# A hybrid decoder layer on one core: the attention's value products of both query groups stand behind the transposes and masked copies of both groups

## The chip, the cores and the metric

The kernel runs on one core of a Trainium2 chip. The metric is the device time of one execution in microseconds (us), and lower is better. The kernel before took 2198.51 us as the median of three runs, which lie between 2198.18 and 2198.69 us. The engines are named as in the profile: PE does matrix products (PEld is its weight load), DVE and ACT do elementwise work, POOL and SP do almost none here beside constants and the issue of transfers.

## The reference

One decoder layer works on 2048 tokens of width 1024. After an RMSNorm and an input projection, four heads of a gated linear recurrence (HGRN2) and eight heads of sliding-window attention run side by side on the same input; their outputs, put side by side, pass an output projection and are added to the residual. A gated MLP with a short causal convolution follows, and a last RMSNorm. The part that the change touches is the attention:

```
scores = jnp.einsum('bnqhgd,bnkhd->bnhgqk', qb, kb) * scale
scores = jnp.where(mask[None, :, None, None], scores, -jnp.inf)
m = jnp.maximum(jnp.max(scores, axis=-1, keepdims=True), sink)
p = jnp.exp(scores - m)
denom = jnp.sum(p, axis=-1, keepdims=True) + jnp.exp(sink - m)
out = jnp.einsum('bnhgqk,bnkhd->bnqhgd', p / denom, vb)
```

Each block of 128 queries reads its own block of 128 keys and the one before it. The recurrence runs beside it:

```
decay = jnp.exp(jnp.where(causal, rel, -jnp.inf))
scores = jnp.einsum('bhtk,bhsk,bhtsk->bhts', qi, ki, decay)
intra = jnp.einsum('bhts,bhsv->bhtv', scores, vi)
inter = jnp.einsum('bhtk,bhkv->bhtv', qi * jnp.exp(b), state)
```

## The kernel before

The 2048 tokens are worked in two halves of 1024. For each half there is first a mixing stage (the loop at line 1187 up to line 1227), then the output projection (`out_proj`), then the gate and up products (`gate_up`), then the down product (`down`). Every large float32 product is made of three products of a high and a low part (hi·hi, hi·lo, lo·hi), so a projection of 128 output columns over 1024 inputs and 1024 tokens is a `unit` (line 194): 8 input tiles (kt) times 3 products times 2 halves of 512 tokens, 48 matmuls of 128x512. In the mixing stage the units f, hq, g (recurrence), q (attention) and, for pairs of heads, pvv (values) fill PE; the output projection's units are called pop. PE executes what it is given in order, and so do DVE and ACT.

In the mixing stage one loop pass per head index h runs two generators side by side, `hgrn` for recurrence head h and `attend` for the head pair (h, h+4) of the attention, and calls `next` on them in a fixed pattern of steps (lines 1198 to 1226). The written order gives each instruction its rank; a scheduler, which runs when the program is built and simulates the engines' times, sets the order on every engine by that rank and by what it thinks ready (`schedule_with_timeline_sim=True`, line 1290). So the place of a `yield` moves ranks, and the built order shows where the instructions went.

`attend` has these parts:

- The q unit, scaled and biased into `qT`, and a `yield`.
- For each of two groups g of four query blocks: the high and low parts `qh` and `ql` (tag `pp`), the score products psc (L459), the copies into `sc`, the row maximum, the exponentials (L481, each 128x128), the division by the sum (L486). Then a `yield`.
- For each group: four transposes of `sc` into the bank ppt (L495) for each of two key/value heads, the masked copies `po` and `pp` from it (L498, tag `pp`, four buffers), the 16 value products into the bank poT (L506; 14 for the very first group), and the copy out of poT: L510 for h below 3; for h = 3, where the result goes straight into the output projection, the high part XH on ACT (L516) and the low part XL on DVE (L517). A `yield` after each group.

The banks psc, ppt, poT and pv share one tag `at` with two buffers in PSUM, and `out_proj` takes both of them for its third unit (d = 2).

`hgrn` walks seven levels m = 1, 2, 4, ... 64 (line 590). At each level PE makes plev from Q and K (L569 for heads 0 to 2, L602 and L607 for head 3), and then DVE changes Q and K in place (L609, L610), which the next level's products read; a masked copy (L625) places the result into `ST`. After the levels come the transposes pkn of K (L640), the copy `Kn` on ACT (L641), the products pu (L647), a chain of eight small sums SS on DVE (L651), the output products po (L665, L666) with a square on ACT for each (L667), a short series of tiny DVE operations for the inverse root (`rsqrt`, line 160), the scaling `on` (L674), the transposes pot (L679), and the result `hg` (L680), which for head 3 is split into XH (L683) and XL (L684).

The output projection's units read the eight mixed tiles in the order kt = 0, 4, 1, 5, 2, 6, 7, 3. Tile 7 comes from the attention of head index 3, and tile 3 from the recurrence of head 3. So in the pass h = 3 the units pop of d = 0, 1 (`pop_3557` and `pop_3558`, `pop_3626` and `pop_3627` in the first half) can run before the mixing is done, except for their steps kt = 7 and kt = 3, and d = 2 (`pop_3697`, `pop_3698`) is tied by the table `BEHIND` (line 38) to stand behind pu, po and pot at its steps 0, 2 and 5.

Of the kernel before, what the change touches and what calls it, by code (L numbers as in the profile page):

```python
# [8 lines left out]
F32 = mybir.dt.float32  # L9
F32R = mybir.dt.float32r  # L10
# [7 lines left out]
P = 128  # L18
# [26 lines left out]
WARM = 12  # L45
TAIL_WARM = 7
LV = 4


@with_exitstack  # L50
def hymba_layer(ctx: ExitStack, tc: tile.TileContext, a: dict, out: bass.AP):
    nc = tc.nc

    def pool(name, bufs=1, space=None, stack=ctx, **kw):
        if space is not None:
            kw["space"] = space
        return stack.enter_context(tc.tile_pool(name=name, bufs=bufs, **kw))
# [12 lines left out]
    def ps(kind, name):  # L70
        return spaces[kind].tile([P, 512], F32, tag=kind, name=name)
# [3 lines left out]
    def halves():  # L75
        return [(b, slice(b * 512, (b + 1) * 512)) for b in range(NB)]
# [117 lines left out]
    def unit(src, X, name, order=range(KT), kind="mm", then={}, behind={}, in_turn=False):  # L194


        hi, lo = src if isinstance(src, tuple) else prep(src)
        o = [ps(aux[b] if kind == "aux" else kind, f"{name}{b}") for b in range(NB)]
        order, mark = list(order), None
        for both in [[h] for h in halves()] if in_turn else [halves()]:  # L200
            for i, kt in enumerate(order):
                if i in then:
                    then[i]()
                wh, wl = hi[:, kt * P:(kt + 1) * P], lo[:, kt * P:(kt + 1) * P]
                xh, xl = X[kt]
                if i in behind:
                    mark = marks[behind[i]].ins
                with tc.issue_after(mark) if mark else ExitStack():
                    for w, x, f, l in ((wh, xh, kt == order[0], False), (wh, xl, False, False),
                                       (wl, xh, False, kt == order[-1])):  # L210
                        for b, bs in both:
                            marks["unit"] = nc.tensor.matmul(o[b], w, x[:, bs], start=f, stop=l)  # L212
        return o

    def new_x():
        return (xp.tile([P, HALF], F32R, tag="xh", name="XH", bufs=KT),
                xp.tile([P, HALF], F32R, tag="xl", name="XL", bufs=KT))
# [74 lines left out]
    def slot(name):  # L292
        return hp.tile([P, HALF], F32, tag="m", name=name, bufs=KT)
# [102 lines left out]
    def rows(kv):  # L396
        return slice(kv * HD, (kv + 1) * HD)
# [32 lines left out]
    def attend(hf, j, X, invb, KS, V, mix, p):  # L430

        o = unit(a["w_att"][j], X, "q")
        qT = slot(f"att{j}")
        for b, bs in halves():
            nc.vector.scalar_tensor_tensor(qT[:, bs], o[b], 0.125, invb[:, bs], op0=ALU.mult, op1=ALU.mult)
            nc.scalar.activation(qT[:, bs], qT[:, bs], AF.Identity, bias=C.bq[:, j:j + 1])
        yield
        scs = []
        for g in range(NB):
            sc = p.tile([P, 2, 4, P], F32, tag="sc", name="sc", bufs=2)  # L440
            gs = slice(g * 512, (g + 1) * 512)
            for kv in range(2):
                r, other = rows(kv), rows(1 - kv)

                qh, ql = [p.tile([P, 512], F32R, tag="pp", name=n, bufs=4) for n in ("qh", "ql")]
                nc.scalar.copy(qh[r], qT[r, gs])
                nc.scalar.copy(qh[other], qT[r, gs])
                nc.vector.tensor_tensor(ql[r], qT[r, gs], qh[r].bitcast(F32), op=ALU.subtract)
                nc.scalar.copy(ql[other], ql[r].bitcast(F32))
                for i0 in (0, 2):  # L450
                    pb = ps("at", "psc")
                    first = hf == 0 and g == 0 and i0 == 0
                    for i in range(2):
                        n = g * 4 + i0 + i
                        w0 = 1 if first and i == 0 else 0
                        o = pb[:, i * 256 + w0 * P:(i + 1) * 256]
                        ks = slice((n + w0) * P, (n + 2) * P)
                        for t, qx in enumerate((qh, ql)):
                            nc.tensor.matmul(o, qx[:, (i0 + i) * P:(i0 + i + 1) * P], KS[:, kv, ks],  # L459
                                             start=t == 0, stop=t == 1)  # L460
                    pv = pb.rearrange("p (i w k) -> p i w k", i=2, w=2)
                    dst = sc[:, kv, i0:i0 + 2]
                    if first:
                        nc.vector.memset(dst[:, 0], NEG)
                        nc.scalar.copy(dst[:, 1], pv[:, 1, 0])
                    else:
                        nc.scalar.copy(dst, pv[:, :, 0])
                    nc.vector.copy_predicated(
                        dst, C.own.bitcast(U32).unsqueeze(1).to_broadcast([P, 2, P]), pv[:, :, 1])
            m = p.tile([P, 2, 4], F32, tag="mx", name="m", bufs=2)  # L470
            nc.vector.tensor_reduce(m.rearrange("p a b -> p (a b)"),
                                    sc.rearrange("p a b c -> p (a b) c"), axis=AX.X, op=ALU.max)
            sk = C.sinkb[:, j].unsqueeze(2).to_broadcast([P, 2, 4])
            nc.vector.tensor_tensor(m, m, sk, op=ALU.max)
            es = p.tile([P, 2, 4], F32, tag="es", name="es", bufs=2)
            nc.vector.tensor_tensor(es, sk, m, op=ALU.subtract)
            nc.vector.tensor_scalar(m, m, -1.0, None, op0=ALU.mult)
            den = p.tile([P, 2, 4], F32, tag="den", name="den", bufs=2)
            for kv in range(2):
                for i in range(4):  # L480
                    nc.scalar.activation(sc[:, kv, i], sc[:, kv, i], AF.Exp, bias=m[:, kv, i:i + 1],  # L481
                                         accum_out=den[:, kv, i:i + 1])
            nc.scalar.activation(es, es, AF.Exp)
            nc.vector.tensor_tensor(den, den, es, op=ALU.add)
            nc.vector.reciprocal(den, den)
            nc.vector.tensor_tensor(sc, sc, den.unsqueeze(3).to_broadcast([P, 2, 4, P]), op=ALU.mult)  # L486
            scs.append(sc)
        yield
        for g, sc in enumerate(scs):
            pm = []  # L490
            for kv in range(2):
                pm.append([p.tile([P, 4, P], F32, tag="pp", name=n, bufs=4) for n in ("po", "pp")])
                pt = ps("at", "ppt")
                for i in range(4):
                    nc.tensor.transpose(pt[:, i * P:(i + 1) * P], sc[:, kv, i], ident)  # L495
                ptv = pt.rearrange("p (i q) -> p i q", i=4)
                for dst, mk in zip(pm[kv], (C.ownT, C.prevT)):
                    nc.vector.tensor_tensor(dst, ptv, mk.unsqueeze(1).to_broadcast([P, 4, P]), op=ALU.mult)  # L498
            oT = ps("at", "poT")
            for i in range(4):  # L500
                n = g * 4 + i
                noprev = hf == 0 and n == 0
                for prev in range(1 if noprev else 2):
                    for kv in range(2):
                        r = rows(kv)
                        nc.tensor.matmul(oT[r, i * P:(i + 1) * P], V[:, n + 1 - prev, r], pm[kv][prev][:, i],  # L506
                                         start=prev == 0, stop=noprev or prev == 1)
            gs = slice(g * 512, (g + 1) * 512)
            if j < ATT_J - 1:
                nc.scalar.copy(qT[:, gs], oT)  # L510
                mix[4 + j] = qT
            else:
                if g == 0:
                    mix[4 + j] = new_x()
                h, l = mix[4 + j]
                nc.scalar.copy(h[:, gs], oT)  # L516
                nc.vector.tensor_tensor(l[:, gs], oT, h[:, gs].bitcast(F32), op=ALU.subtract)  # L517
            yield

    def hgrn(hf, h, X, invb, vs, WG, mix, p, fu=None):  # L520

# [50 lines left out]
        def place_pairs():  # L572

            plv = pl.rearrange("p (r c t) -> p r c t", r=TT // 2, c=2)
            moved, odd = [p.tile([P, TT // 2, 64], F32, tag="lv", name=n, bufs=LV) for n in ("moved", "odd")]
            nc.scalar.copy(moved, plv[:, :, 1])
# [610 lines left out]
    for hf in range(NH):  # L1187
        X, kv, invb, rs, f0 = nxt
        with ExitStack() as st:
            p = pool(f"mix{hf}", stack=st, reuse_waits="tile")  # L1190
# [37 lines left out]
        with ExitStack() as st:  # L1228
            p = pool(f"ffn{hf}", stack=st, reuse_waits="tile")
# [64 lines left out]
```

## Time and profile before

| | |
|---|---|
| timed runs | 2198.18 to 2198.69 us, median 2198.51 |
| profiled execution, first to last instruction | 2198.0 us (its own time is not given apart from this span) |
| PE busy | 2180.4 us, 99% |
| DVE busy | 1639.5 us, 75% |
| ACT busy | 1049.9 us, 48% |
| chain that ended last | PE 95%, DVE 3%, ACT 1%, DMA 1% |
| heads 0 to 2 of the mixing, from the first plev to the first pop | 90.2 to 334.2 us and 1180.0 to 1424.6 us |
| head 3, with the output projection's first three units, to the first pop of the fourth | 334.2 to 404.2 us and 1424.6 to 1494.2 us |

In the profile's lists a line reads: start in us, duration in us, engine, line of the kernel, operation, out<-in, shape, how many of them in a row, and in brackets how long the engine sat idle before it and what ended that. Matmuls overlap by their pipeline, so the distance from start to start tells what one costs. A float32 product of small tiles appears as two records. A list by windows shows for each stretch its length and the busy time of the engines in it, with the number of instructions, and then the granted TensorE clock (PEclk) as a share of the full one.

### The profile page before, as it was taken

The page shows a single profiled execution, that of the slowest core. Times are in us where ns is not written, and L with a number is a line of the kernel's source. Part 1 is how long each engine was busy: PE and PEld are TensorE (multiplying, and loading weights), DVE is VectorE, ACT ScalarE, POOL GpSimd, SP SyncE. Part 2 cuts the span into 40 slices and gives each one's busy share as a digit, 9 for nine tenths or more (in the row PEclk, how much of TensorE's full clock was granted, in tenths as well). Part 3 has the DMA queues.
Part 4 walks back from the last instruction along what each step waited for, and adds up shares of the span by engine and source line. Part 5 has one row for each costly group of instructions (what it writes and reads, how often), then busy time and mean ns, then how long its engine had stood idle before and what let it go on. Part 6 is the DMA issues. An engine that isn't in the chain of part 4 may idle for free.

```text
span 2198.0 us, 29524 instructions
## 1 busy us (share of the span) xinstructions
PE 2180.4 (99%) x11424; PEld 1834.0 (83%) x11424; DVE 1639.5 (75%) x2451; ACT 1049.9 (48%) x1848; POOL 6.3 (0%) x28
## 2 busy tenths in 40 slices
PE   9999999999999999999999999999999999999998
PEld 7988988888888888888889889888888888888888
DVE  6567568688887888885855666677888878887766
ACT  6445544454444445335735455544644444443353
POOL 1000000000000000000000000000000000000000
PEclk9999999999999999999999999999999999999999
DMA  4101112323333234964631111114132323259643
GB/s 155 51 32 48 39 41 68 119 74 102 104 109 108 89 127 143 372 241 156 209 125 41 44 36 51 58 39 134 58 125 92 125 91 109 98 183 393 233 144 130
DMA packets 94358, 257.91 MB, mean 117 GB/s; under 512 B 11594, under 2 KB 17546, under 8 KB 94218
## 3 DMA queue, kind: packets, MB, share of 16 engines
q1 hardware_dynamic: 88992, 251.30, 33.9%
q10 hardware_dynamic: 5226, 4.73, 0.7%
q8 instruction: 89, 1.46, 0.3%
q14 instruction: 51, 0.42, 0.1%
HBM read 195.10 MB, written 57.15 MB: 115 GB/s over the span
## 4 chain that ended last, share of the span: by engine, by line
PE 95%; DVE 3%; ACT 1%; DMA 1%; issue 0%; SPq 0%; DVEq 0%; ACTq 0%
PE X L877 7%; PE X L878 7%; PE X L879 7%; PE pop L212 7%; PE hq L212 4%; PE q L212 4%; PE f L212 4%; PE g L212 4%; PE Y L879 4%; PE Y L878 4%; PE Y L877 4%; PE pdx L1088 3%; PE pdx L1089 3%; PE pdx L1090 3%; PE pdy L1089 3%; PE pdy L1088 3%
## 5 line engine op out<-in xcount | busy, mean ns | idle before, releaser
L706 ACT CAST whi<-raw 128x1024 fp32r<-128x1024 f32 x88 | 92.6, 1053 | 109.2 <-PE X L878 68.2
L877 PE MATMUL X<-T,whi 128*128 128x512 f32 x352 | 136.9, 389 | 0.0
L878 PE MATMUL X<-T,whi 128*128 128x512 f32 x352 | 136.9, 389 | 0.0
L879 PE MATMUL X<-T,wlo 128*128 128x512 f32 x352 | 136.9, 389 | 0.0
L972 DVE SCALAR_TENSOR_TENSOR y<-ga,cw,y 128x1024 f32<-128x1024 f32 x88 | 112.5, 1281 | 26.0 <-ACT y L970 26.0
L884 ACT COPY u<-X 128x512 f32<-128x512 f32 x88 | 51.4, 585 | 133.3 <-PE X L879 133.1
L707 DVE TENSOR_TENSOR wlo<-raw,whi 128x1024 fp32r<-128x1024 f32 x88 | 107.3, 1220 | 0.0
L190 ACT CAST whi<-raw 128x1024 fp32r<-128x1024 f32 x57 | 59.5, 1048 | 93.1 <-PE q L212 31.9
L707 DVE TENSOR_TENSOR xld<-raw,xhd 128x1024 fp32r<-128x1024 f32 x72 | 80.8, 1133 | 19.1 <-ACT xhd L706 18.9
L706 ACT CAST xhd<-raw 128x1024 fp32r<-128x1024 f32 x72 | 69.7, 978 | 43.6 <-DMA raw<-act0T 14.8
L212 PE MATMUL pop<-XL,whi 128*128 128x512 f32 x256 | 86.1, 396 | 2.1 <-DVE XL L224 2.1
L212 PE MATMUL pop<-XH,wlo 128*128 128x512 f32 x256 | 85.2, 393 | 0.8 <-DVE wlo L191 0.8
L212 PE MATMUL pop<-XH,whi 128*128 128x512 f32 x256 | 84.5, 397 | 0.2
L878 PEld LDWEIGHTS X<-T,whi 128*128 128x128 f32 x352 | 66.1, 188 | 13.7
L877 PEld LDWEIGHTS X<-T,whi 128*128 128x128 f32 x352 | 66.1, 188 | 13.7
L879 PEld LDWEIGHTS X<-T,wlo 128*128 128x128 f32 x352 | 66.1, 188 | 13.7
L1088 PE MATMUL pdx<-xhd,hid 128*128 128x512 f32 x192 | 74.4, 391 | 1.0 <-ACT hid L706 1.0
L1089 PE MATMUL pdx<-xld,hid 128*128 128x512 f32 x192 | 74.7, 389 | 0.0
L1090 PE MATMUL pdx<-xhd,lod 128*128 128x512 f32 x192 | 73.7, 389 | 0.0
L698 PE MATMUL pvv<-whi,XH 128*128 128x256 f32 x256 | 73.5, 288 | 0.0
L191 DVE TENSOR_TENSOR wlo<-raw,whi 128x1024 fp32r<-128x1024 f32 x57 | 69.5, 1222 | 4.2 <-ACT whi L190 4.1
L699 PE MATMUL pvv<-whi,XL 128*128 128x256 f32 x256 | 72.6, 284 | 0.0
(379 smaller groups left out, 6563.3 us busy)
## 6 DMA issues: line engine op xcount, KB each, us to landing
wr<-in_w_down SPq DMA_DIRECT2D x90, 512.0 KB, 4.8
raw<-in_w_gate SPq DMA_DIRECT2D x44, 512.0 KB, 3.6
raw<-in_w_up SPq DMA_DIRECT2D x44, 512.0 KB, 3.6
raw<-act0T SPq DMA_DIRECT2D x20, 512.0 KB, 6.1
raw<-act1T SPq DMA_DIRECT2D x20, 512.0 KB, 10.1
act0B<-y SPq DMA_DIRECT2D x33, 256.0 KB, 2.6
act1B<-y SPq DMA_DIRECT2D x33, 256.0 KB, 2.4
raw<-in_w_out SPq DMA_DIRECT2D x16, 512.0 KB, 4.7
```

The source lines that it names most:

```text
L212: marks["unit"] = nc.tensor.matmul(o[b], w, x[:, bs], start=f, stop=l)
L698: nc.tensor.matmul(o[:, 0:256], xh[:, t], hi[:, c], start=kt == 0, stop=False)
L699: nc.tensor.matmul(o[:, 0:256], xl[:, t], hi[:, c], start=False, stop=False)
L706: return (nc.scalar.copy(h, src), (eng or nc.vector).tensor_tensor(l, src, h.bitcast(F32), op=ALU.subtract))
L707: (eng or nc.vector).tensor_tensor(l, src, h.bitcast(F32), op=ALU.subtract))
L877: nc.tensor.matmul(o, wh[:, ws], xh, start=i == 0 and not more, stop=False, skip_group_check=more)
L878: nc.tensor.matmul(o, wh[:, ws], xl, start=False, stop=False, skip_group_check=more)
L879: r = nc.tensor.matmul(o, wl[:, ws], xh, start=False, stop=i == 3, skip_group_check=more)
L972: nc.vector.scalar_tensor_tensor(y, g[:, w:w + HALF], C.cw[:, ft, w:w + 1], y, op0=ALU.mult, op1=ALU.add)
L1088: nc.tensor.matmul(o, wh[:, i, c], ah[:, i, cols], start=f, stop=False, skip_group_check=more)
L1089: nc.tensor.matmul(o, wh[:, i, c], al[:, i, cols], start=False, stop=False, skip_group_check=more)
L1090: nc.tensor.matmul(o, wl[:, i, c], ah[:, i, cols], start=False, stop=l, skip_group_check=more)
```

## The change

The loop over groups in `attend` is cut in two. The first loop makes the transposes and masked copies of both groups and keeps their tiles in `pms`; then there is a `yield`; the second loop makes the value products and the copies out of poT of both groups; then there is one `yield` where there was one per group. The number of yields is the same, so the calls of `next` around it stay as they are. The tag `pp` has eight buffers (PB) in place of four, which the eight masked copies of both groups need at once; `qh` and `ql` use the same tag and have the eight too. The four further buffers are 2 KB per partition each. The program is built with `dynamic_dma_scratch_size=1024`.

For h below 3 both parts still follow each other in the written order (apart from what stands between two `next` calls). For h = 3 the third `next(at)` now holds the transposes and masked copies of both groups, and the fourth holds all value products and the copies L516 and L517 (here L521 and L522) of both groups, behind the last step of `hgrn` with po, pot and hg.

```
+PB = 8
...
-                qh, ql = [p.tile([P, 512], F32R, tag="pp", name=n, bufs=4) for n in ("qh", "ql")]
+                qh, ql = [p.tile([P, 512], F32R, tag="pp", name=n, bufs=PB) for n in ("qh", "ql")]
...
         yield
+        pms = []
         for g, sc in enumerate(scs):
             pm = []
+            pms.append(pm)
             for kv in range(2):
-                pm.append([p.tile([P, 4, P], F32, tag="pp", name=n, bufs=4) for n in ("po", "pp")])
+                pm.append([p.tile([P, 4, P], F32, tag="pp", name=n, bufs=PB) for n in ("po", "pp")])
                 pt = ps("at", "ppt")
...
+        yield
+        for g, pm in enumerate(pms):
             oT = ps("at", "poT")
...
                 nc.vector.tensor_tensor(l[:, gs], oT, h[:, gs].bitcast(F32), op=ALU.subtract)
-            yield
+        yield
...
-    nc = bacc.Bacc("TRN2", target_bir_lowering=False, num_devices=1)
+    nc = bacc.Bacc("TRN2", target_bir_lowering=False, num_devices=1, dynamic_dma_scratch_size=1024)
```

No instruction is added or removed on PE, DVE, POOL and SP; ACT gets two further loads of an activation table (in the passes of the second half), since exponentials and sigmoids stand in another order. Line numbers of the changed kernel are larger by one to five. The order of the built programs shows three places.

First, PE in the first half, pass h = 3, from the fifth level's plev on. Before, matmuls of the output projection (pop, 128x512) stand between the short products:

```order
L602 MATMUL plev<-Q,K 128x64 x8
L212 MATMUL pop_3557<-XH,whi 128x512
L212 MATMUL pop_3626<-XH,whi 128x512
L495 MATMUL ppt<-ident,sc 128x128 x4
L506 MATMUL poT<-po,V 64x128
L212 MATMUL pop_3557<-XL,whi 128x512
L212 MATMUL pop_3557<-XH,wlo 128x512
L212 MATMUL pop_3626<-XL,whi 128x512
L212 MATMUL pop_3626<-XH,wlo 128x512
L607 MATMUL plev<-Q,K 32x32 x16
```

Six more pop stand there ahead of pkn, twelve between pu and po, and eighteen between po and pot. In the changed kernel the same place reads, from the last value products to the start of po:

```order
L511 MATMUL poT<-pp,V 64x128 x2
L612 MATMUL plev<-Q,K 32x32 x16
L612 MATMUL plev<-Q,K 64x64 x8
L645 MATMUL pkn<-ident,K 128x128 x8
L652 MATMUL pu<-v,Kn 128x128 x8
L670 MATMUL po<-v,ST 128x128
L671 MATMUL po<-state,Q 128x128
```

and from the last po on:

```order
L670 MATMUL po<-v,ST 128x128
L671 MATMUL po<-SS,Q 128x128
L684 MATMUL pot<-ident,on 128x128 x8
L213 MATMUL pop_3557<-XH,whi 128x512
L213 MATMUL pop_3626<-XH,whi 128x512
L213 MATMUL pop_3558<-XH,whi 128x512
L213 MATMUL pop_3627<-XH,whi 128x512
```

All 42 pop that stood between the third level's plev and pot are now behind pot (in the second half 49, of which seven moved ahead of the third level's plev). No pop stands between the third level's plev and pot any more.

Second, DVE and ACT at the end of the same pass. Before, DVE forms XL of the attention's first group among the levels:

```order
L498 TENSOR_TENSOR po<-ppt,ownT 128x512
L498 TENSOR_TENSOR pp<-ppt,prevT 128x512
L517 TENSOR_TENSOR XL<-poT,XH 128x512
L609 TENSOR_TENSOR Q<-Q,f 128x32x16
L610 TENSOR_TENSOR K<-K,f 128x32x16
```

In the changed kernel both XL of the attention are among the last of the pass, behind `on` and `hg`:

```order
L679 TENSOR_TENSOR on<-po,y 128x512 x2
L685 SCALAR_TENSOR_TENSOR hg_2970<-pot,hgw,hg_2970 128x512 x2
L689 TENSOR_TENSOR XL<-hg_2970,XH 128x512
L522 TENSOR_TENSOR XL<-poT,XH 128x512 x2
L689 TENSOR_TENSOR XL<-hg_2970,XH 128x512
```

and on ACT both copies XH from poT stand behind the first XH of `hg`:

```order
L646 COPY Kn<-pkn 128x512 x2
L672 ACTIVATE on,ss<-po 128x128 x8
L688 CAST XH<-hg_2970 128x512
L521 CAST XH<-poT 128x512 x2
L688 CAST XH<-hg_2970 128x512
```

The four copies of tile 7 moved from the levels to behind the recurrence's result, so what reads tile 7 on PE comes later than the recurrence.

Third, PE in the pass h = 0 of the first half, beside the hq unit. Before, single value products are split off from their run:

```order
L212 MATMUL hq_1373<-XL,whi 128x512
L212 MATMUL hq_1372<-XH,wlo 128x512
L506 MATMUL poT<-po,V 64x128
L665 MATMUL po<-v,ST 128x128
L666 MATMUL po<-SS,Q 128x128
L212 MATMUL hq_1373<-XH,wlo 128x512
```

In the changed kernel the value products of both groups stand in one run, whose start is:

```order
L213 MATMUL hq_1372<-XH,whi 128x512
L213 MATMUL hq_1373<-XH,whi 128x512
L511 MATMUL poT<-po,V 64x128 x4
L511 MATMUL poT<-pp,V 64x128 x2
L511 MATMUL poT<-po,V 64x128 x2
L511 MATMUL poT<-pp,V 64x128 x2
```

In the passes h = 0 to 2 of both halves the value products stood in 25 runs of 1 to 16; now they stand in 6 runs of 30 or 32.

## The prediction

> **What bounds the kernel now.** I read the page's list of engines and its chain first, then windows over the two mixing stages, and last the lists by time of PE, DVE and ACT around the places whose order changes.
>
> ```profile
> PE 2180.4 (99%) x11424; PEld 1834.0 (83%) x11424; DVE 1639.5 (75%) x2451; ACT 1049.9 (48%) x1848; POOL 6.3 (0%) x28
> PE 95%; DVE 3%; ACT 1%; DMA 1%; issue 0%; SPq 0%; DVEq 0%; ACTq 0%
> ```
> ```profile
> 117.00:324.00 207.00, 207.00 (x1387) 178.55 (x1386) 133.10 (x263) 101.90 (x265) 0.00 (x0) 1.00 0.13 40
> ...
> 362.30:381.60 19.30, 18.57 (x185) 15.23 (x183) 16.89 (x32) 2.67 (x7) 0.00 (x0) 0.91 0.00 1
> 381.60:392.00 10.40, 10.02 (x69) 8.73 (x69) 3.01 (x9) 3.46 (x16) 0.00 (x0) 1.00 0.01 2
> ```
>
> PE is never short of work: it is the whole chain but for 5%. In heads 0 to 2 (first window) it has no idle time at all, so there only a cheaper PE row can gain. In head 3 (the next two windows) it is idle for 0.73 + 0.38 us only, while DVE is busy for 16.89 of 19.30 us: the recurrence is a chain PE–DVE–PE there, and PE is full because the pop fill its waits. PE runs in its built order, so a pop that stands behind a waiting product fills nothing. That is what the change touches.
>
> **Part one: the tail of head 3.** The first half, by time:
>
> ```profile
> 362.30 1.89 PE L602 MATMUL plev<-Q,K 128*128 128x64 f32 x16
> ...
> 381.65 1.07 PE L640 MATMUL pkn<-ident,K 128*128 128x128 f32 x8
> 382.95 2.05 PE L647 MATMUL pu<-v,Kn 128*128 128x128 f32 x16 [0.24 <-ACT Kn L641]
> 384.76 0.70 PE L212 MATMUL pop<-XH,whi 128*128 128x512 f32 x2
> ...
> 387.61 0.38 PE L665 MATMUL po<-v,ST 128*128 128x128 f32 x2
> ...
> 391.99 0.70 PE L212 MATMUL pop<-XH,whi 128*128 128x512 f32 x2
> ...
> 394.36 0.62 PE L212 MATMUL pop<-XH,wlo 128*128 128x512 f32 x2
> ...
> 396.18 1.03 PE L679 MATMUL pot<-ident,on 128*128 128x128 f32 x8
> 396.97 0.71 PE L212 MATMUL pop<-XH,whi 128*128 128x512 f32 x2
> ```
> ```profile
> 364.32 0.68 DVE L609 TENSOR_TENSOR Q<-Q,f 128x512 f32<-128x512 f32 x1
> ...
> 394.89 1.29 DVE L674 TENSOR_TENSOR on<-po,y 128x512 f32<-128x512 f32 x2
> 396.82 1.41 DVE L680 SCALAR_TENSOR_TENSOR hg<-pot,hgw,hg 128x512 f32<-128x512 f32 x2 [0.64 <-PE pot L679]
> ```
> ```profile
> 379.00 0.58 ACT L516 CAST XH<-poT 128x512 fp32r<-128x512 f32 x1 [1.29 <-PE poT L506]
> ...
> 397.60 1.28 ACT L683 CAST XH<-hg 128x512 fp32r<-128x512 f32 x2 [4.97 <-DVE hg L680]
> ```
>
> From plev to the end of pot (362.30 to 396.97) PE also does 42 pop. One costs 0.2275 us (eight from 394.36 to 396.18), so 9.55 us. The changed order has all 42 behind pot, so I rebuild the chain without them, from the Q copy at 364.32, which waits for neither. The masked copies of both groups are eight by about 0.6 us, as before (the distance of such DVE rows), two XL of 0.6 leave, and the value products wait for them; walking the changed DVE and PE orders with the durations above puts pkn at 380.45, 1.2 earlier than 381.65. The rest is a chain whose steps keep their length: pkn to pu 1.30 (381.65 to 382.95), pu 1.81 (to 384.76), then po at once, since the three us of pop that ended at 387.61 are gone: 383.55. From the first po to the first pop behind it 4.38 (387.61 to 391.99; ACT's squares set that), and 4.19 more to pot (396.18: DVE's small operations and `on`). So pot runs from 392.1 to 392.9. The first pop behind it reads tile 7, whose XH now stands on ACT behind the first XH of hg: 0.64 from the start of pot to hg, 0.7 for hg, 0.64 for its XH (1.28 for two), 0.58 for XH of poT: 394.8. Then the 42 pop cost their 9.55 and reach 404.35 where they reached 396.97: **+7.4 us**. What is late next is XL of poT behind the XL of hg; four pop of 0.9 us cover all but some tenths of it, and I add nothing.
>
> The second half has the same chain:
>
> ```profile
> 1452.70 1.89 PE L602 MATMUL plev<-Q,K 128*128 128x64 f32 x16
> ...
> 1486.25 1.03 PE L679 MATMUL pot<-ident,on 128*128 128x128 f32 x8
> ```
>
> Before, pot ends at 1487.04 (0.79 later, as in the first half), with 49 pop inside. Seven of them now stand ahead of that plev: 1.6 us, so it starts at 1454.3, is done 1.7 later, and the Q copy follows at 1456.0, when DVE is free anyway. The same 30.5 us (364.32 to 394.8) bring the first pop to 1486.6, the other 42 reach 1496.1: **+9.1 us**. Ends for the two together: 11.5 and 21.5, if the walked orders (who waits for a bank of tag `at`, and when DVE takes which copy) are wrong by 2.5 us a half.
>
> **Part two: waits that go.** The pop moved back or forth meet their inputs later than these were ready.
>
> ```profile
> 344.31 1.16 PE L544 MATMUL pdiag<-hg,K 128*128 128x128 f32 x8 [0.35 <-DVE hg L680]
> ...
> 350.76 0.74 PE L212 MATMUL pop<-XL,whi 128*128 128x512 f32 x2 [0.70 <-DVE XL L224]
> ...
> 1439.84 1.06 PE L212 MATMUL pop<-XL,whi 128*128 128x512 f32 x2 [1.39 <-DVE XL L224]
> ...
> 1493.71 0.39 PE L212 MATMUL pop<-XH,wlo 128*128 128x512 f32 x1
> 1494.22 0.73 PE L212 MATMUL pop<-XH,whi 128*128 128x512 f32 x2
> ...
> 1495.73 0.61 PE L212 MATMUL pop<-XL,whi 128*128 128x512 f32 x2
> 1496.74 0.73 PE L212 MATMUL pop<-XH,wlo 128*128 128x512 f32 x2 [0.40 <-DVE wlo L191]
> ```
>
> The XL at line 224 come earlier in the changed DVE order, so 0.35 + 0.70 and 1.39 us go. At 1494.22 the fourth unit waits 0.28 (0.51 from the row ahead, less 0.23) and at 1496.74 it waits 0.55 (1.01 less two pop); the first half has the same two waits. With 10 us more in front the weights are there: 2 x 0.83. The half clock behind 1440 (next part) goes with its wait: 1.7. Together **-5.8 us**, with ends of 0 and -5.8, since each can come back at another row.
>
> **Part three: value products of heads 0 to 2.** They stood in 25 runs and stand in 6.
>
> ```profile
> 142.69 0.39 PE L212 MATMUL hq<-XH,whi 128*128 128x512 f32 x1
> 143.01 0.43 PE L506 MATMUL poT<-po,V 128*64 128x128 f32 x2
> 143.37 0.50 PE L212 MATMUL hq<-XH,whi 128*128 128x512 f32 x1
> 143.71 0.39 PE L212 MATMUL hq<-XL,whi 128*128 128x512 f32 x1
> ```
> ```profile
> 145.48 1.89 PE poT L506 x30
> ```
>
> One product (two records) alone between two hq: from 142.69 to 143.71 are 1.02 us for it and two hq of 0.2275, so it costs 0.57. In a run it costs 1.89 / 15 = 0.13. Nineteen joins at 0.44 are 8.4 us; many pieces were longer, or lay at the end of other small products, where an edge is paid anyway. I take two thirds, **-6 us**, with ends of -3 and, if the joined product were free, -10.8 (19 x 0.57).
>
> **Part four: the clock.** PE now waits long between short products.
>
> ```profile
> 364.90:368.30 3.40, 2.72 (x24) 2.30 (x24) 3.40 (x8) 0.00 (x0) 0.00 (x0) 0.99 0.00 0
> 368.30:371.70 3.40, 3.40 (x28) 2.74 (x25) 2.58 (x6) 0.31 (x1) 0.00 (x0) 0.50 0.00 0
> 1436.60:1440.00 3.40, 2.01 (x15) 1.71 (x15) 3.40 (x5) 2.31 (x5) 0.00 (x0) 1.00 0.16 65
> 1440.00:1443.50 3.50, 3.50 (x9) 2.72 (x10) 3.50 (x7) 0.00 (x0) 0.00 (x0) 0.51 0.68 165
> ```
> ```profile
> 367.72 3.63 PE poT L506 x28
> ```
>
> After 3.4 us with 0.68 us idle, and again after 3.4 us with 1.39 us idle, the granted clock was 0.5 for the next 3.4 us; the 28 value products in it took 3.63 us, where 30 at the full clock took 1.89: 1.7 us lost. In the changed tail I count three stretches a half that are emptier than these: the levels between 364 and 373, the last levels up to pkn, and the wait from po over pot to the first pop, in which 6.9 us hold 0.8 us of products. Six stretches of 1.7 are 10.2; part of the slowed products lies in waits, so I take **+9 us**, ends 0 and 16 (about half of each tail slow, and the first 3.4 us of pop behind it).
>
> [...]
>
> **What costs nothing.** No DMA issue is among the moved instructions, and the four further buffers hold no transfer's target; DMA takes at most 0.02 of the tail's windows above. The two more table loads on ACT lie in heads 0 to 2, where ACT is busy for half the time. The scratch size reserves memory alone; no queue that uses it shows in the profile.
>
> **Sum.** 7.4 + 9.1 - 5.8 - 6 + 9 = +13.7 us on the profiled span of 2198.0, which is 0.5 below the median of the runs: 2212.2 us, slower by 0.6%.
>
> **Rivals.** (1) The clock falls only behind the longest wait, from the end of po to pot, 4.2 us of nothing a half: one window of 1.7 each, 3.4 in place of 9, **2206.6 us**. For it, the clock stayed full from 381.6 to 392.0 with 0.38 us idle, so not every gap costs; against it, the two windows above. [...] (2) The clock stays low through both tails, so that the doubled products lie on the chain: 11 stretches of 1.7, 19 in place of 9, **2222 us**. For it, PE is under half busy there; against it, each low stretch of before lasted 3.4 us and ended. (3) Not slower: the joins pay in full and the clock holds. The place is the poT runs of heads 0 to 2; the price is 19 x 0.57 = 10.8. Then 16.5 - 5.8 - 10.8 + 0 is about 0: **2198.4 us**. With no clock loss it decides from 0.33 us a join on (6.3 us, which leaves +4.4). For it, PE is full there and each gain counts; against it, the tails' 16.5 us is worth 49 + 42 pop that lose their cover. (4) Eight masked copies ahead of the first value product make PE wait in heads 0 to 2 (DVE is busy for 133 of 207 us there): some 0.7 us in six passes, +4, **2216 us**. That the change doesn't do what it says is excluded by the built order.
>
> **How the numbers follow.** About 4.4 us (0.2%) is what a measurement of this kernel can tell from no change. The forecast's case (2209 to 2218, the clock term between 5 and 14) has 0.47; rival 1 (2203 to 2209) 0.20; rival 2 (2218 to 2227) 0.13; rival 3 (2196 to 2203) 0.12, with 0.03 of it faster than 2194.1; rival 4 0.08. So faster 0.03, same 0.10, slower 0.87. The range leaves out most of rival 3 and the upper part of rival 2: 2202 to 2224.
>
> **What would show it.** Right: no pop between the third level's plev and pot in either half; PE idle 4 us ahead of pot and 2 us behind it (released by DVE `on`, then ACT XH of poT); pot to the fourth unit's first pop some 10 us longer; granted clock under 1 in several windows of 364 to 398 and 1456 to 1490; poT in one run of about 1.9 us a group in heads 0 to 2, and these heads shorter by about 3 us a half. Wrong: heads 0 to 2 as long as before or shorter by 5 us a half; the clock full through the tails; pkn later than 381, which would mean a longer chain than I walked.

## The result

The changed kernel takes 2217.18 us in the median of four runs (2215.61 to 2218.23), the kernel before 2198.35 (2198.05 to 2198.69). The ratio is 1.0087, with a 95% interval of 1.0075 to 1.0098: slower by 18.8 us.

The profiled run took 2215.61 us and has a span of 2213.9. In every run of the kernel before and of the changed kernel that lists both times, 1.7 to 1.8 us lie around the span. So the profile before, with its span of 2198.0, stands for a run of about 2199.7 and not of 2198.5, as the prediction took it; the two spans differ by 15.9 us.

The page of the changed kernel, engines and chain:

```profile
PE 2175.2 (98%) x11424; PEld 1837.4 (83%) x11424; DVE 1640.6 (74%) x2451; ACT 1054.3 (48%) x1850; POOL 6.0 (0%) x28
PE 94%; DVE 4%; ACT 1%; DMA 1%; issue 0%; SPq 0%; DVEq 0%; ACTq 0%
```

PE is busy for 5 us less than before, over a span that is 16 longer: the loss is idle time of PE, not added work (a part of what remains is slower, by the clock, as shown below). Its list of waits names it (us in total, times, longest):

```profile
PE pot L684 <- DVE on L679: 6.8, 2, 3.4
PE plev L612 <- DVE f L621: 3.0, 2, 1.5
PE pkn L645 <- DVE K L615: 3.0, 2, 1.5
PE poT L511 <- DVE pp L501: 2.9, 2, 1.5
PE pop L213 <- ACT XH L521: 2.4, 2, 1.3
PE po L670 <- ACT on L672: 1.9, 4, 0.5
...
PE po L670 <- DVE SS L656: 1.4, 2, 0.7
```

Each stands once or twice in each half's tail of head 3. By time, in the first half and at the two ends of the second:

```profile
357.67 1.89 PE L607 MATMUL plev<-Q,K 128*128 128x64 f32 x16
...
376.55 1.06 PE L645 MATMUL pkn<-ident,K 128*128 128x128 f32 x8 [1.48 <-DVE K L615]
377.85 2.05 PE L652 MATMUL pu<-v,Kn 128*128 128x128 f32 x16 [0.24 <-ACT Kn L646]
380.60 0.49 PE L670 MATMUL po<-v,ST 128*128 128x128 f32 x2 [0.70 <-DVE SS L656]
...
389.89 1.32 PE L684 MATMUL pot<-ident,on 128*128 128x128 f32 x8 [3.40 <-DVE on L679]
392.53 2.08 PE L213 MATMUL pop<-XH,whi 128*128 128x512 f32 x4 [1.32 <-ACT XH L521]
```
```profile
1454.73 1.89 PE L607 MATMUL plev<-Q,K 128*128 128x64 f32 x16
...
1491.77 2.07 PE L213 MATMUL pop<-XH,whi 128*128 128x512 f32 x4 [1.12 <-ACT XH L521]
```

From the third level's plev to the first pop behind pot are 34.86 us (357.67 to 392.53), without one pop inside. Before there were 34.67 (362.30 to 396.97) with 42 pop inside. The chain kept its length and lost its filling. The same stretch in windows (length, then busy time of PE, PEld, DVE, ACT, POOL, then the granted clock):

```profile
117.00:324.00 207.00, 207.00 (x1410) 182.11 (x1408) 136.48 (x267) 105.70 (x272) 0.00 (x0) 1.00 0.15 43
357.67:376.55 18.88, 13.15 (x174) 11.92 (x172) 15.85 (x30) 1.76 (x6) 0.00 (x0) 1.00 0.00 1
376.55:389.89 13.34, 8.01 (x56) 6.63 (x56) 5.59 (x22) 4.02 (x18) 0.00 (x0) 1.00 0.00 1
387.70:391.10 3.40, 1.18 (x8) 0.83 (x8) 2.98 (x11) 0.00 (x0) 0.00 (x0) 1.00 0.01 2
391.10:397.90 6.80, 5.48 (x14) 4.21 (x14) 4.08 (x7) 2.51 (x5) 0.00 (x0) 0.50 0.28 80
1459.50:1462.90 3.40, 1.78 (x15) 1.33 (x14) 3.40 (x7) 0.00 (x0) 0.00 (x0) 1.00 0.00 0
1462.90:1466.30 3.40, 2.98 (x28) 3.01 (x30) 2.85 (x6) 0.00 (x0) 0.00 (x0) 0.50 0.02 5
1483.40:1486.80 3.40, 1.41 (x11) 1.02 (x9) 0.93 (x6) 1.10 (x6) 0.00 (x0) 1.00 0.00 0
1486.80:1497.00 10.20, 7.21 (x20) 5.70 (x21) 6.79 (x15) 2.38 (x5) 0.00 (x0) 0.50 0.18 51
```

PE is idle for 5.7 and 5.3 us in the second and third windows, where it was idle for 0.7 and 0.4. The half clock follows three times in the tails, for 6.8, 3.4 and 10.2 us, each time behind 3.4 us in which PE was busy for 1.2 to 1.8.

The gain is in heads 0 to 2, whose first window is as full of PE as before. Their ends, before and after (first plev of head 0, first pop of head 3, first product of the gate):

```profile
73.64 0.28 PE L569 MATMUL plev<-Q,KK 128*128 128x128 f32 x1
...
334.24 0.39 PE L212 MATMUL pop<-XH,whi 128*128 128x512 f32 x1
...
459.39 0.39 PE L877 MATMUL X<-B,whi 128*128 128x512 f32 x1
```
```profile
73.86 0.28 PE L574 MATMUL plev<-Q,KK 128*128 128x128 f32 x1
...
330.62 0.40 PE L213 MATMUL pop<-XH,whi 128*128 128x512 f32 x1
...
465.93 0.39 PE L882 MATMUL X<-B,whi 128*128 128x512 f32 x1
```

(The table ahead calls 90.2 and 1180.0 us the first plev; the first ones stand at 73.64 and 1163.50.) The account of the two spans, each stretch taken between such rows:

| stretch | first half | second half |
|---|---|---|
| heads 0 to 2: first plev to first pop | 260.60 to 256.76: -3.84 | 261.11 to 257.43: -3.68 |
| first pop to the third level's plev of head 3 | 28.06 to 27.05: -1.01 | 28.09 to 27.04: -1.05 |
| third level's plev to the first pop behind pot | 34.67 to 34.86: +0.19 | 34.34 to 37.04: +2.70 |
| that pop to the first product of the gate | 62.42 to 73.40: +10.98 | 62.43 to 73.32: +10.89 |

Together +15.2; the remaining 0.7 us is spread over the other stages.

### The profile page after: what moved, and what is told of

It reads as the page before. It is cut to its first block, busy times and chain, and to the rows that moved or that the text cites. A ratio compares the mean times of both kernels' runs of the same rounds, so it can differ in the third digit from the quotient of the medians.

```text
span 2213.9 us, 29507 instructions
## 1 busy us (share of the span) xinstructions
PE 2175.2 (98%) x11424; PEld 1837.4 (83%) x11424; DVE 1640.6 (74%) x2451; ACT 1054.3 (48%) x1850; POOL 6.0 (0%) x28
## 4 chain that ended last, share of the span: by engine, by line
PE 94%; DVE 4%; ACT 1%; DMA 1%; issue 0%; SPq 0%; DVEq 0%; ACTq 0%
PE X L882 7%; PE X L883 7%; PE X L884 7%; PE pop L213 7%; PE f L213 4%; PE hq L213 4%; PE q L213 4%; PE Y L884 4%; PE Y L882 4%; PE Y L883 4%; PE g L213 3%; PE pdx L1093 3%; PE pdx L1095 3%; PE pdx L1094 3%; PE pdy L1093 3%; PE pdy L1095 3%
## 5 line engine op out<-in xcount | busy, mean ns | idle before, releaser
L884 PEld LDWEIGHTS X<-T,wlo 128*128 128x128 f32 x352 | 66.1, 188 | 13.7
L882 PEld LDWEIGHTS X<-T,whi 128*128 128x128 f32 x352 | 66.1, 188 | 13.7
```

The costliest lines, as they stand in the source:

```text
L882: nc.tensor.matmul(o, wh[:, ws], xh, start=i == 0 and not more, stop=False, skip_group_check=more)
L884: r = nc.tensor.matmul(o, wl[:, ws], xh, start=False, stop=i == 3, skip_group_check=more)
```

## The experiments

**Where the loss and the gain lie.** Two kernels give the new loops to a part of the heads. The first:

```
+        if j < ATT_J - 1:
             pms = []
...
+        else:
+            for g, sc in enumerate(scs):
...
+                yield
```

> Head index 3 has the old loop (each group's transposes, copies and value products together), heads 0 to 2 the new one. Theory A (the loss is the lost cover in head 3, the gain lies in heads 0 to 2): the 42 and 49 pop are back between the levels and pot, so the loss is gone and the gain of heads 0 to 2 (7.5 us by the two profiles) and some 2 us of shorter waits before the tail stay: 2189 to 2192 us. Theory B (the gain of heads 0 to 2 exists only because PE reaches the tail earlier and waits there instead): 2196 to 2199 us.

It took 2188.81 us (2187.54 to 2190.11), a ratio to before of 0.9954 (0.9939 to 0.9969): the fastest kernel of this study, 10.0 us under the kernel before and 28.4 under the changed one. Its windows over the tail of the first half, cut at the same instructions as above:

```profile
357.62:376.08 18.46, 17.36 (x185) 14.22 (x184) 17.03 (x32) 2.94 (x8) 0.00 (x0) 1.00 0.00 1
376.08:390.62 14.54, 14.21 (x86) 12.10 (x87) 6.15 (x22) 4.02 (x18) 0.00 (x0) 1.00 0.01 2
```

The tail is full again, and its clock never falls. Heads 0 to 2 are as short as in the changed kernel (-3.84 and -3.68 us). Theory A holds.

The second has the two branches the other way round (`if j == ATT_J - 1` for the new loops).

> The reverse: heads 0 to 2 have the old loop, head 3 the new one. Theory A: all of the loss and none of the gain, 2217.2 + 7.5 = 2224.7, between 2223 and 2227 us. Theory B, or a loss that heads 0 to 2 share: 2214 to 2219 us.

It took 2224.28 us (2221.72 to 2224.91; ratio 1.0112, 1.0095 to 1.0129). Theory A again: the loss is there in full, the gain is not.

**Place or grouping.** In the changed kernel the work of both groups in head 3 is both grouped and late. Two kernels take these apart; in both, heads 0 to 2 are new. The first is grouped but early:

```
-        yield
+        if j < ATT_J - 1:
+            yield
         for g, pm in enumerate(pms):
...
         yield
+        if j == ATT_J - 1:
+            yield
```

> All heads have the new loops, but for head 3 the yield between them is left out and an empty step is put behind: copies and value products of both groups are written in the third step, ahead of the last step of the recurrence. Theory A (place, not grouping): the order has 42 pop in the first tail again, 2189 to 2194 us. Rival C (eight masked copies in a row on DVE hold up the recurrence's copies of Q and K): pkn comes 2 us or more later in each half and the time is 2196 to 2204 us.

It took 2194.57 us (2191.87 to 2195.76; ratio 0.9978, 0.9969 to 0.9988), between the two ranges. The 42 pop are back, as theory A has it; but from the third level's plev to pkn are 20.48 us in the first half and 22.35 in the second, where the first experiment has 18.46 and 18.27, so pkn comes later by the 2 us or more that rival C names (3.4 us of the second half's stretch are at the half clock). The other is group by group but late: for head 3 a `yield` stands ahead of the old loop, and none between its groups.

> Heads 0 to 2 new; head 3 has the old loop, group by group, but both groups are written in the fourth step, behind the last step of the recurrence, and the third step is empty. The order has no pop between the third level's plev and pot in the first tail. Theory A (the place of tile 7 costs the cover; the grouping costs 2 to 3 us a half, as the third experiment has against the first): close to the changed kernel less the grouping, 2209 to 2217 us. Rival C (the grouping of the copies is the larger part): near the third experiment or below, 2190 to 2197 us.

It took 2213.17 us (2212.53 to 2215.38; ratio 1.0065, 1.0050 to 1.0080). With the first experiment (early, group by group, 2188.81) and the changed kernel (late, grouped, 2217.18) these four make a square. Lateness costs 24.4 us group by group and 22.6 grouped; grouping costs 5.8 us early and 4.0 late. So place is the larger cause, but rival C holds in part. What grouping costs shows in the waits of the grouped and early kernel:

```profile
PE pkn L648 <- DVE K L618: 3.0, 2, 1.5
PE poT L512 <- DVE pp L501: 2.9, 2, 1.5
```

Neither is among the longer waits of the first experiment's kernel. The value products wait here for the sixth of the eight masked copies (they share two banks with the transposes, all of which now stand ahead), and no pop stands between the last level's products and pkn, where the first experiment has six.

**What the buffers do alone.** The kernel before with `bufs=8` for both uses of `pp` and the scratch size:

```
-                qh, ql = [p.tile([P, 512], F32R, tag="pp", name=n, bufs=4) for n in ("qh", "ql")]
+                qh, ql = [p.tile([P, 512], F32R, tag="pp", name=n, bufs=8) for n in ("qh", "ql")]
...
-                pm.append([p.tile([P, 4, P], F32, tag="pp", name=n, bufs=4) for n in ("po", "pp")])
+                pm.append([p.tile([P, 4, P], F32, tag="pp", name=n, bufs=8) for n in ("po", "pp")])
```

> The kernel before with eight buffers for tag pp and the scratch size, and nothing else. Theory A: value products still stand in 12 runs a half in place of 3, so no gain: 2197 to 2200 us. Rival D (the gain of heads 0 to 2 comes from the buffers, through qh and ql and the score products): 2190 to 2193 us.

It took 2193.79 us (2192.71 to 2196.58; ratio 0.9979, 0.9970 to 0.9989). My theory missed this gain of 5 us, and rival D's range ends 0.8 us below the time. The gain lies only in part where rival D put it: by its profile heads 0 to 2 gain 1.6 us in the first half and lose 0.1 in the second, and head 3 with the output projection gains 1.5 and 2.0, in which two half-clock stretches of before (at 368.3 and 1440.0 us) are gone. Another 1.5 us of that profile's gain lies outside the mixing, at a third such stretch of before, and says nothing of the change. The joined runs come from the loops alone: with the buffers the value products of heads 0 to 2 stand in 30 runs, five more than before, and with the loops in 6. In all kernels with the eight buffers these heads take 259.0 and 261.2 us with the old loops and 256.8 and 257.4 with the new ones, so the loops are worth 6.0 us. This kernel also completes a square with the first two experiments and the changed kernel, all four with eight buffers: by the medians the new loops in heads 0 to 2 gain 5.0 us (2193.79 to 2188.81) or 7.1 (2224.28 to 2217.18), and in head 3 they cost 28.4 or 30.5. A run of value products in head 0 with the buffers, then with the loops too (start, length, count of records, from the chain):

```profile
145.43 1.67 PE poT L506 x26
```
```profile
140.52 3.43 PE poT L511 x60
...
1236.72 3.65 PE poT L511 x64
```

And the scratch size alone (one argument at the build, no instruction moved):

> The kernel before with the scratch size alone; the order on every engine is that of before. Theory A: no change, 2197 to 2200 us. Rival G (the gain of the fourth experiment comes from the scratch size and the placement in memory that follows from it): 2192 to 2195 us.

2199.45 us (ratio 1.0001, 0.9992 to 1.0010). It does nothing; the buffers do it. Its profile shows the order of before a second time, and here the clock is full at both places in head 3 where the profile before had the half clock; only the stretch outside the mixing is there again (at 1108.3). Yet its span is 2198.4 us against 2198.0. From head 3's first pop to the gate the second half takes 124.84 us here, with the clock full, and 124.86 in the profile before, with the half clock at 1440.0: that stretch cost nothing, and the buffers' 2.0 us there are not the clock's. The first half takes 123.96 us against 125.15, so 1.2 of the 1.5 us there are not shown to be the buffers'.

**What the third unit's products are worth as cover.** The first experiment's kernel with one table entry changed:

```
-BEHIND = {1: {0: 1}, 2: {0: "pu", 2: "po", 5: "pot"}}
+BEHIND = {1: {0: 1}, 2: {0: "pot"}}
```

> The first experiment's kernel, in which the 42 pop are back, with one line of BEHIND changed: the third unit (d = 2) stands as a whole behind pot, so 30 of the 42 pop (12 between pu and po, 18 between po and pot) leave the tail; tile 7 and its 12 pop among the levels stay where they are. Theory A, with the share of these 30: 0.7 + 0.5 + 0.5 us idle ahead of and in po and 3.4 us ahead of pot come back in each half, 10 us for both, and one or two half-clock windows a half at 1.2 to 1.7 us: 2201 to 2206 us. Rival H (what counts is tile 7 alone, and the products of d = 2 are as well done later, since PE is then never short): 2188 to 2192 us.

It took 2200.61 us (2198.43 to 2202.49; ratio 1.0006, 0.9997 to 1.0016), 11.8 more than the first experiment and 0.4 under theory A's range. Its waits and the windows at pot:

```profile
PE pot L716 <- DVE on L711: 6.8, 2, 3.4
PE po L702 <- ACT on L704: 2.0, 4, 0.5
...
PE po L702 <- DVE SS L688: 1.4, 2, 0.7
```
```profile
384.60:388.00 3.40, 0.71 (x4) 0.52 (x4) 1.51 (x9) 0.73 (x4) 0.00 (x0) 0.99 0.00 0
388.00:394.80 6.80, 5.65 (x18) 4.77 (x19) 4.41 (x8) 1.24 (x2) 0.00 (x0) 0.50 0.06 7
```

The same three waits as in the changed kernel, to 0.1 us. Without these 30 pop the stretch from the third level's plev to the first pop behind pot shrinks by only 0.34 us (33.79 to 33.45): they had cost the chain little. (0.8 us of the stretch are pot at the half clock, with 1.62 us from pot to the first pop where the first experiment has 0.79; without it the chain would be some 1.2 us shorter, an estimate.) If the parts add, which no run tests, then of the 28.4 us between the first experiment and the changed kernel, 11.8 go with the third unit's 30 pop and the half clock that follows their leaving; 4.0 to 5.8 are the grouping; the other 11 to 13 go with the late tile 7, its 12 pop, the wait for its XH and the rest of the clock, which no run here takes apart.

**Other filling for the same waits.** The changed kernel with 30 pop of the second unit held back for the waits:

```
-BEHIND = {1: {0: 1}, 2: {0: "pu", 2: "po", 5: "pot"}}
+BEHIND = {1: {0: 1, 1: 16, 2: "pu", 3: "po"}, 2: {0: "pu", 2: "po", 5: "pot"}}
```

> The changed kernel with 30 pop of the second unit held back by the table BEHIND: 6 behind the level 16, 6 behind pu and 18 behind po. Tile 7 comes as late as in the changed kernel. Theory A (what was lost is cover, so any pop in the waits gives it back): about 30 x 0.2275 = 6.8 us a half less idle time, less 1 us where the 18 are longer than the wait, and two of three half-clock windows a half gone: 2198 to 2206 us. Rival E (the chain itself got longer by tile 7 being last, and filling it only moves the waits to the front): 2213 to 2218 us.

It took 2214.69 us (2213.25 to 2217.21; ratio 1.0071, 1.0056 to 1.0086). That is 2.5 us under the changed kernel, in rival E's range and not in mine. By the two profiles nothing of it lies in the tails: from head 3's first pop to the gate the halves are together 0.5 us longer, and the 2.5 us lie between the halves, where this profile has no half-clock stretch. The wait ahead of pot is gone, but a new one stands first among the waits, ahead of the third level, where the held pop had been, and the clock goes down behind it:

```profile
PE plev L607 <- DVE es L477: 6.3, 2, 3.1
```
```profile
349.40:352.80 3.40, 2.11 (x16) 1.63 (x14) 3.40 (x6) 1.20 (x7) 0.00 (x0) 1.00 0.01 4
352.80:373.30 20.50, 17.18 (x88) 15.89 (x90) 15.09 (x31) 5.28 (x28) 0.00 (x0) 0.50 0.00 1
```

Rival E's mechanism is only a part of this. PE's idle time between the third level's plev and the first pop behind pot fell from 12.4 to 5.7 us in the first half and from 12.2 to 6.9 in the second, and 3.5 us came back ahead of it in each half. Most of the rest went with the slowed clock: from the third level's plev to pkn this kernel takes 24.89 and 24.30 us, the changed kernel 18.88 and 20.53. So the 72 pop that can run before tile 7 are already cover where they stand, and moving some moves a part of the wait; what they would give with the clock full is not shown.

**The clock.** The changed kernel with 12 extra products of zero weights, added into the first unit's banks between po and pot (`zero` is a tile of zeros, and `fill` is 12 for the first unit):

```
+                if fill and i == 6:
+                    with tc.issue_after(marks["po"].ins):
+                        for n in range(fill):
+                            b, bs = halves()[n % NB]
+                            nc.tensor.matmul(o[b], zero, X[0][0][:, bs], start=False, stop=False)
```

> The changed kernel with 12 extra products of zero weights (128x512, added into the banks of the first pop unit, so that nothing changes in value) between po and pot of head 3 in each half, where PE is idle for 3.4 us. 12 x 0.2275 = 2.7 us fit in. Theory A with the clock term: the half-clock windows behind pot (6.8 and 10.2 us long in the profile) go or get shorter, 2 to 3 us a half: 2210 to 2214 us. Rival F (the clock falls because of the levels before, or the low stretch behind pot costs nothing): 2216 to 2219 us.

It took 2212.33 us (2210.11 to 2212.94; ratio 1.0060, 1.0043 to 1.0077). More products, and 4.9 us less. The windows behind pot, which had the half clock:

```profile
391.00:394.40 3.40, 2.05 (x11) 1.40 (x11) 3.23 (x6) 2.11 (x4) 0.00 (x0) 1.00 0.00 0
394.40:397.80 3.40, 3.40 (x16) 2.80 (x15) 2.04 (x4) 0.63 (x1) 0.00 (x0) 1.00 0.42 92
...
1487.30:1490.70 3.40, 3.24 (x8) 2.56 (x9) 2.15 (x4) 1.12 (x3) 0.00 (x0) 0.50 0.05 7
1490.70:1494.10 3.40, 3.40 (x16) 2.78 (x15) 1.38 (x2) 0.63 (x1) 0.00 (x0) 1.00 0.64 230
```

In the first half it is full now (3.4 us at 0.5 stand earlier instead, from 378.0); in the second 3.4 us of 10.2 are left. Rival F falls: with the wait ahead of pot filled, the clock behind it stays full in the first half and is low for a third as long in the second. From head 3's first pop to the gate the two halves are 1.7 and 1.2 us shorter than in the changed kernel. Another 2.1 of the 5.5 us between the two spans lie between the halves, where the profile of the changed kernel has a half-clock stretch (at 1114.7) and this one has none; so 2.9 us are shown at the place of the edit.

## Why the prediction was right, and where its terms were off

The direction, the place and the cause were right, and 2217.18 lies in the range of 2202 to 2224; the forecast of 2212.2 was 5.0 short. That it came so near is in part luck, since too short a chain (4.9 us) stands against a clock term that was too large (2.4) and a gain that was too small (1.5). By its steps, against the account above:

- **Heads 0 to 2** (forecast -6): -7.5. The six runs stand as forecast, and the loops give 6.0 of it, the -7.5 less the 1.5 of the buffers alone. That 1.5, with the buffers' further gain in head 3, is an effect that the prediction, which gave the buffers no effect of their own, left out.
- **Waits ahead of the tail** (forecast -5.8 with those at the fourth unit and the clock behind 1440): right in sign. The third level's plev came 1.0 us earlier in each half, in the second with seven pop (1.6 us) more ahead of it.
- **The chain without pop.** This step failed. I let the chain get shorter when its 42 pop left: 32.5 us from plev to the first pop in the first half, and 32.3 in the second. It took 34.86 and 37.04. In the first half pkn came 18.88 us behind plev where I had walked 18.15, po 4.05 behind pkn where I had 3.10, pot 9.29 behind po where I had 8.57. The new rows of waits say why for po and pot: po waits 0.70 for SS and 0.52 and 0.46 for ACT, waits which the pop had hidden and which I had therefore not seen. The kernel from whose tails only the third unit's 30 pop are gone has the same waits in po, and the same 9.29 from po to pot where the first experiment has 8.57. Ahead of pkn the last levels and pkn wait 1.49 and 1.48 for DVE; the prediction does not say how much of this its walk had. The step's error is 2.4 us in the first half and 4.7 in the second, where 2.2 of it are the half clock over the value products and pot (37.04 less 34.86).
- **42 pop behind pot** (9.55 us a half): right. From the first pop behind pot to the gate both halves grew by 10.98 and 10.89, which is the 9.55, less 0.83 for the two waits at the fourth unit, which went, and plus 2.2 for the half clock. Where this clock is full (both halves with the held products, the first with the zero products) the stretch takes 70.92 us in place of 73.40 and 73.32, so the half clock is worth 2.4 to 2.5 there.
- **The clock** (forecast +9 from six stretches): six windows of 3.4 us at 0.5 is what the profile has (6.8 + 3.4 + 10.2 = 20.4 us), but their places differ: one among the levels and five around pot, in place of four and two. Their price is about 6.6 us: 2.2 behind pot in each half, and the 2.2 by which the second half's chain is longer than the first's. The clock fell behind windows with PE busy for 1.18, 1.78 and 1.41 of 3.40 us. Behind the zero products it stayed full in the first half; ahead of the held products it fell behind 3.40 us with PE busy for 2.11 and stayed at 0.5 for 20.5 us with PE busy for 17.18. What makes it fall, or come back, no run here shows.
- **Rivals.** The case of a clock that falls only behind the longest wait (2206.6) and the not-slower case (2198.4) were wrong; the latter's gain in heads 0 to 2, 6.0 us by the loops and 7.5 with the buffers, came near the 6.3 from which it would have decided, at 0.25 us a join (6.0 / 24, from 30 runs to 6), but the clock did not hold and the chain was 4.9 us longer than its sum has it. Products of heads 0 to 2 that starve did not show: PE is busy for all 207 us there. The case of a clock that stays low through both tails was nearer in time (2222) than in mechanism.

The profiles' difference is 15.9 us against 13.7 forecast: +4.9 from the longer chain without the clock, -2.4 from the clock term, -1.5 from heads 0 to 2, +0.5 ahead of the tail and +0.7 from the other stages. The other 3 us of the medians' 18.8 are the runs that the two profiles caught: that of the changed kernel is its fastest of four, with a granted clock of 0.994 where the others have 0.992, and that of before is 1.3 us above its median.

## What to carry to other kernels

When independent products fill the waits of a chain on a full engine, removing them need not shorten the chain: here 30 of them left in each half and it shrank by 0.34 us, while their 6.8 us came back behind it. So when a reorder joins work that belongs together, look at which banks and results are released later by it, and what products wait for those; here the same edit gained in three heads and lost in the fourth, and limiting it to the three beat both kernels by 10.0 and 28.4 us (5.0 of the 10.0 are the buffers'). A buffer that an edit needs may carry a gain of its own and is worth a run alone.

## What was not expected of the hardware

Twelve products with zero weights, placed in an idle stretch of each half, made the whole kernel 4.9 us faster; the granted clock is the only gain that its profile shows at their place. And a clock that had fallen stayed down though PE was mostly busy: in the kernel with held products it was 0.5 for 20.5 us, in which PE was busy for 17.18 us by the slowed records. Nor did PE's busy time alone tell here when the clock fell: in the profile before it fell behind 3.4 us with PE busy for 2.01 (from 1436.6), and with the same order in the kernel with the scratch size it stayed full behind 3.4 us with PE busy for 2.05 (from 1436.2).
